# Seven-product units: one product over all of K at a time, with partial results passed from PSUM bank to PSUM bank

## The chip, the cores and the metric

The kernel runs on one core of one Trainium2 chip. Its engines work side by side and meet only at semaphores: PE (TensorE, matmuls; PEld is its weight load), DVE (VectorE) and ACT (ScalarE) for elementwise work, POOL (GpSimd) and SP (SyncE), which here issue transfers. SBUF is the working memory, PSUM the eight banks that matmuls add into, each 128 partitions x 512 float32. The metric is device time in microseconds (us): the median of the runs of one kernel.

## The reference

One encoder layer on x of 512 tokens x 2048, in float32. `h = rmsnorm(x)` is projected by `w_in` (2048 x 6176) to attention and gated-linear-attention operands; the two mixers' outputs go through `w_out` and are added to x; then a gated feed-forward part and a last norm:

```python
h = rmsnorm(x, attn_norm_w[l])
proj = h @ w_in[l]
aq, ak, av, gq, gk, gv, gr, glr = jnp.split(proj, split_idx, axis=-1)
...
x = x + mixed
h = rmsnorm(x, ffn_norm_w[l])
x = x + (jax.nn.silu(h @ w_gate[l]) * (h @ w_up[l])) @ w_down[l]
return rmsnorm(x, final_norm_w)
```

`w_gate` and `w_up` are 2048 x 5632. The change touches how 16 blocks of 256 columns of `w_in` (gates, GLA queries and keys, attention queries and keys) and the 44 blocks of 256 columns of `w_gate` and `w_up` are multiplied.

## The kernel before

**Numbers.** A float32 operand is split into a rounded high part (ACT, a cast to fp32r) and the rest (DVE, a subtraction). A product is high x high + high x low + low x high.

**Units of seven products.** A unit gives 256 output columns x 512 tokens. Tokens are cut into two halves of 256, columns into two halves of 128, and K = 2048 into eight pairs of 128-row tiles, so each pair is a 2 x 2 block product; Winograd's form does it with seven products instead of eight, on sums and differences of blocks. The token side (`B11`, `T1`, `T2`, `B21`, `T3`, `B22`, `T4`, for each of the eight pairs, high and low side by side) is made once and stays in SBUF. The weight side is made for every unit. One product of one pair is a wide matmul (512 columns: the high weights times the high and low tokens, L1603) and a narrow one (256 columns: the low weights times the high tokens, L1589), 112 matmuls a unit. There are 58 such units: 16 in `Front` (the first projection) and 42 in `Feed` (gate and up in turn; its first two units, u = 0 and 1, go by another, narrower form).

**Pieces.** A unit runs over K in four pieces of two pairs. Per piece, one 512 KB load of 4 x 128 rows x 256 columns (1024 bytes to a row, L1474 on SP), three DVE operations for block sums (L1493 to L1495), two casts (L1506) and two subtractions (L1511), 768 and 1024 elements; then all seven products for the piece. Seven PSUM banks take one product each, and all four pieces add into them. In `Feed` one piece in eight has its sums made ahead: generator `ahead` makes them between the matmuls of the out-projection (DVE, L1563) and writes them to HBM (`sd`, L1565, POOL), and they are read back in place of the sums (L1573).

**Eviction.** After the fourth piece `evac7` reads the seven banks: nine ACT copies and seven DVE additions and subtractions of 256 columns, then the remaining additions as four accumulating transfers on POOL (L1648, L1649, L1654, L1655), and a last DVE addition. `finish` multiplies by the norm's row, in `Front` writes the result to HBM from POOL (`grd`, `gfd`, `qkd`, L1757), in `Feed` applies silu to the gate and multiplies it with up, and writes `gd` (L1699), once for two units.

**Order and buffers.** The program's text sets each engine's order; nothing is rescheduled. Generators put into `urgent` are moved on by one step each time `run_urgent` is called, between pieces. SBUF is handed out in numbered slots: `s2` (names a0 to a35, 2 KB to a partition) and `s4` (b0 to b32, 4 KB). `put` returns a slot at the end of a first-in, first-out list and `get` takes the first, when the program is written, so who uses a slot next is fixed, and the next user waits at a semaphore for the last one. A slot that is being written out to HBM can be taken at once, and its next user then waits for that transfer. A wait stands in an engine's queue, and what is behind it waits too. The token operands fill much of `s4` in `Front`.

## Time and profile before

| | us |
|---|---|
| median of 3 runs | 2141.43 (2138.18 to 2142.17) |
| the profiled execution | 2140.3 |
| its span | 2138.5 |
| PE busy | 2126.0 |
| DVE busy | 1826.6 |
| ACT busy | 1264.8 |
| POOL busy | 388.7 |

The span runs from the first instruction to the last; the profiled execution's own time is 1.8 us longer. A row of a timeline shows start, length, engine, line, operation and output<-input with buffer numbers left out, then how many, and in brackets the idle time ahead of it with what ended it. A row of a grouped view shows the count, the busy time, the mean ns of one, and the idle time ahead of the group with what ended most of it. A row of waits shows us in total, times, and the longest. A row of DMA issues shows the size of one in KB and the median us from issue to landing. "L" and a number is a line of the kernel that the row is of.

### The profile page before, as it was taken

The numbers are of one execution on the slowest core, as the hardware profiler recorded it, in microseconds if no ns is written. First come the engines' busy times: TensorE is split into PE (matmuls) and PEld (weight loads), VectorE is DVE, ScalarE is ACT, GpSimd is POOL, SyncE is SP. The second block draws the span as 40 slices with busy tenths as digits, with TensorE's granted clock in tenths as the row PEclk, the third lists the DMA queues.
The fourth block names the chain that finished last, engine by engine and source line by source line (L and its number), as shares of the span: only waits on it lengthen the run. The fifth ranks groups of instructions, "written<-read, shape, count | busy, mean of one in ns | idle before, by whom it ended". The sixth has DMA issues, their size and how long they took to land.

```text
span 2138.5 us, 32543 instructions
## 1 busy us (share of the span) xinstructions
PE 2126.0 (99%) x11410; PEld 1825.3 (85%) x11410; DVE 1826.6 (85%) x3002; ACT 1264.8 (59%) x2281; POOL 388.7 (18%) x531
## 2 busy tenths in 40 slices
PE   9999999999999999999999999999999999999998
PEld 7888888888888889888888888888888888888887
DVE  5699999888878788899899898998999888887885
ACT  8445555477776546455555555555555666666762
POOL 0011121332222010011221122112121220332000
PEclk9999999999999999999999999999999999999999
DMA  6367777877676773477767777677667897999572
GB/s 205 128 184 181 180 180 184 203 219 212 189 228 209 244 253 108 140 177 183 190 174 184 185 180 186 178 179 196 176 181 187 247 277 248 201 255 249 188 249 79
DMA packets 272369, 416.85 MB, mean 195 GB/s; under 512 B 19853, under 2 KB 164477, under 8 KB 272206
## 3 DMA queue, kind: packets, MB, share of 16 engines
q1 hardware_dynamic: 208926, 280.10, 40.9%
q0 software_dynamic: 62960, 134.15, 29.4%
q8 instruction: 90, 1.47, 0.3%
q14 instruction: 73, 0.60, 0.1%
q10 hardware_dynamic: 320, 0.53, 0.1%
HBM read 289.57 MB, written 71.93 MB: 169 GB/s over the span
## 4 chain that ended last, share of the span: by engine, by line
PE 56%; DVE 1%; DMA 1%; ACT 1%; issue 0%; SPq 0%; DVEq 0%; ACTq 0%
PE ps L1603 25%; PE ps L1589 13%; PE ps L2024 5%; PE ps L2023 5%; PE ps L2025 5%; PE ps L347 1%; PE ps L348 1%; PE ps L346 1%; PE ps L2240 1%; PE ps L2239 1%; PE ps L2238 1%; DMA a<-xd 0%; DMA gd<-b 0%; ACT b L237 0%; DVE a L1847 0%
## 5 line engine op out<-in xcount | busy, mean ns | idle before, releaser
L1506 ACT CAST b<-b 128x1024 fp32r<-128x1024 f32 (+1 forms) x473 | 433.7, 945 | 293.5 <-DVE b L1511 199.9
L1603 PE MATMUL ps<-b,b 128*128 128x512 f32 x1760 | 517.2, 393 | 0.4 <-ACT b L1506 0.2
L1511 DVE TENSOR_TENSOR b<-b,b 128x1024 fp32r<-128x1024 f32 (+1 forms) x473 | 495.7, 1084 | 18.8 <-ACT b L1506 8.9
L1603 PE MATMUL ps<-a,b 128*128 128x512 f32 x1488 | 436.4, 393 | 0.6 <-DVE b L1623 0.6
L1603 PEld LDWEIGHTS ps<-b,b 128*128 128x128 f32 x1760 | 298.1, 188 | 33.2 <-ACT b L1506 0.7
L1589 PEld LDWEIGHTS ps<-b,b 128*128 128x128 f32 x1760 | 289.9, 190 | 42.4
L1589 PE MATMUL ps<-b,b 128*128 128x256 f32 x1760 | 318.0, 280 | 0.0
L1589 PEld LDWEIGHTS ps<-a,b 128*128 128x128 f32 x1488 | 246.6, 189 | 39.2 <-DVE b L1511 0.5
L1603 PEld LDWEIGHTS ps<-a,b 128*128 128x128 f32 x1488 | 248.9, 188 | 25.7 <-ACT b L1506 0.8
L1589 PE MATMUL ps<-a,b 128*128 128x256 f32 x1488 | 267.5, 280 | 0.1
L1999 DVE TENSOR_TENSOR b<-b,b 128x1024 fp32r<-128x1024 f32 x112 | 136.5, 1221 | 31.8 <-ACT b L1991 30.0
L1493 DVE TENSOR_TENSOR b<-b 128x512 f32<-128x512 f32 x212 | 145.2, 685 | 2.4 <-DMA grd<-b 0.9
L346 PE MATMUL ps<-b,b 128*128 128x512 f32 x332 | 134.8, 406 | 0.0
L1991 ACT CAST b<-b 128x1024 fp32r<-128x1024 f32 x112 | 116.6, 1052 | 30.1 <-DVE b L1979 16.4
L348 PE MATMUL ps<-b,b 128*128 128x512 f32 x332 | 130.0, 392 | 0.0
L347 PE MATMUL ps<-b,b 128*128 128x512 f32 x332 | 129.9, 391 | 0.0
L1648 POOL DMA_DIRECT2D b<-a x58 | 50.2, 866 | 413.2 <-ACT b L1506 272.1
L1654 POOL DMA_DIRECT2D b<-a x58 | 50.1, 864 | 285.9 <-DMA b<-a 160.9
L1494 DVE TENSOR_TENSOR b<-b,b 128x256 f32<-128x256 f32 x212 | 90.1, 425 | 7.4
L1495 DVE TENSOR_TENSOR b<-b,b 128x256 f32<-128x256 f32 x212 | 90.2, 425 | 7.3
L218 DVE TENSOR_TENSOR b<-b,b 128x512 fp32r<-128x512 f32 x116 | 77.0, 685 | 20.7 <-ACT b L237 20.5
L1629 ACT COPY a<-ps 128x256 f32<-128x256 f32 x58 | 21.6, 372 | 122.0 <-PE ps L1589 121.8
(313 smaller groups left out, 4215.5 us busy)
## 6 DMA issues: line engine op xcount, KB each, us to landing
b<-in_w_gate_dram SPq DMA_DIRECT2D x109, 512.0 KB, 4.0
b<-in_w_in_dram SPq DMA_DIRECT2D x94, 512.0 KB, 4.0
b<-in_w_up_dram SPq DMA_DIRECT2D x88, 512.0 KB, 3.9
b<-in_w_down_dram SPq DMA_DIRECT2D x88, 512.0 KB, 8.0
b<-a POOLq DMA_DIRECT2D x174, 256.0 KB, 4.5
b<-in_w_out_dram SPq DMA_DIRECT2D x32, 512.0 KB, 4.6
md<-a POOLq DMA_DIRECT2D x56, 256.0 KB, 6.9
gd<-b POOLq DMA_DIRECT2D x22, 512.0 KB, 3.9
```

The costliest lines, as they stand in the source:

```text
L346: mm(o, xh.t[:, c], wh.t[:, w], start=first and not on, stop=False, skip_group_check=on)
L347: mm(o, xh.t[:, c], wl.t[:, w], start=False, stop=False, skip_group_check=on)
L348: mm(o, xl.t[:, c], wh.t[:, w], start=False, stop=last, skip_group_check=on)
L1493: dve.tensor_tensor(s_[:, :, 0:2], r[:, :, 1:3], r[:, :, 0:1].to_broadcast(shape), op=OP.add)
L1506: act.copy(o, src)
L1511: dve.tensor_tensor(o, src, h, op=OP.subtract)
L1589: mm(o, wl, xh, start=False, stop=end, skip_group_check=True)
L1603: mm(o.rearrange("p (s t) -> p s t", s=2), wh, x_, start=first and p == 0, stop=False, skip_group_check=True)
L1991: act.copy(hi.t, self.src[i].t)
L1999: dve.tensor_tensor(lo.t, s.t, hi.f, op=OP.subtract)
L2023: mm(o, xh[:, t], wh, start=new and j == 0, stop=False, skip_group_check=True)
L2024: mm(o, xh[:, t], wl, start=False, stop=False, skip_group_check=True)
```

## The change

**A unit over K.** `Units` replaces the pieces in `Front` and in the 42 units of `Feed`. A unit is seven steps, one product each, and each step runs over all eight pairs: eight wide matmuls, then eight narrow ones, on one bank. The order of products is `B11`, `T1`, `T2`, `B21`, `T3`, `B22`, `T4`.

**Weights by quadrant.** A load (`fetch`, L1531) brings one quadrant of the unit's weights, one of the two row tiles of every pair and one half of the columns: 512 KB, in rows of 512 bytes. Up to eight are held, as long as more than `KEEP` = 3 slots of `s4` stay free. Four DVE additions of 1024 elements a unit make the sums (`add`, L1538), and each step has one cast (`cast`, L1563, ACT) and one subtraction (`sub`, L1569, DVE) of 1024 elements, two steps ahead of its matmuls (`AHEAD`).

**Banks.** The banks are X, V, Y, W and Z. X takes product 0. While PE runs product 1 into V, ACT writes -X into bank Y, and product 2 adds to it; ACT then writes -Y into bank W, DVE writes V - Y into bank Z, and products 4 and 6 add to W, 5 to Z, 3 to X. A bank that no matmul of these units has filled before gets one extra wide matmul first (`seat`). V is copied to SBUF (L1632). A step's eviction (`evac_`) stands in the program behind the casts and sums of the next step. The results are copied by ACT and added by DVE (L1623, L1624) as each bank ends, so the accumulating transfers are gone, and so are `evac7`, `ahead` and `sd`. `Front` now needs all eight pairs of token operands at its start. The products of a unit, the two halves of the result, `finish` and its writes stay.

```diff
@@ pair operands: slots kept by name, so that they can be freed by product @@
-            xi[q] = dict(x_, slots=slots + more)
+            xi[q] = dict(x_, slots=slots)
...
-        class Feed(Blocks):
...
-            def ahead(self):
...
-            def products(self, i, banks):
...
-            def evac7(self, u, banks):
...
+        class Units:
+            ORDER = ("B11", "T1", "T2", "B21", "T3", "B22", "T4")
+            FREES = {0: "B11", 4: "T3", 5: "B22", 6: "T4"}
+            AHEAD, KEEP = 2, 3
+            def open(self, first):
+                self.steps = [(u, n) for u in range(first, len(self.units)) for n in range(7)]
+                self.todo = deque((u, b) for u in range(first, len(self.units)) for b in (2, 0, 1, 3))
+                self.quads, self.sums_, self.his, self.both = {}, {}, {}, {}
+                self.banks, self.outs, self.parts = {}, {}, {}
+                self.late_ = []
+            def fetch(self, most=8):
+                while self.todo and len(self.quads) < most and len(s4.free) > self.KEEP:
+                    u, b = self.todo.popleft()
+                    r = self.quads[u, b] = s4.get(F32, [P, NP, P])
+                    w, col = self.place(u)
+                    k, h = divmod(b, 2)
+                    rows = w[:, col + h * P:col + (h + 1) * P].rearrange("(q k p) c -> k p q c", k=2, p=P)
+                    sp.dma_start(out=r.t, in_=rows[k])
+            def add(self, i):
+                if i >= len(self.steps):
+                    return
+                u, n = self.steps[i]
+                tt = lambda o, x_, y_: dve.tensor_tensor(o.t, x_.t, y_.t, op=OP.add)
+                Q = lambda b: self.quads[u, b]
+                if n == 0:
+                    s_ = self.sums_[u, 1] = s4.get(F32, [P, NP, P])
+                    tt(s_, Q(2), Q(0))
+                if n == 1:
+                    tt(Q(0), Q(0), Q(1))
+                if n == 2:
+                    s_ = self.sums_[u, 2] = s4.get(F32, [P, NP, P])
+                    tt(s_, Q(0), Q(2))
+                if n == 5:
+                    s_ = self.sums_[u, 2]
+                    tt(s_, s_, Q(3))
+                    put(self.quads.pop((u, 3)))
+            def from_(self, i):
+                u, n = self.steps[i]
+                home, key = ((self.quads, 1), (self.sums_, 1), (self.sums_, 2), (self.quads, 3), (self.quads, 0),
+                             (self.sums_, 2), (self.quads, 2))[n]
+                return home, (u, key)
+            def cast(self, i):
+                if i < len(self.steps):
+                    home, key = self.from_(i)
+                    hi = self.his[i] = s4.get(F32R, [P, NP, P])
+                    act.copy(hi.t, home[key].t)
+            def sub(self, i):
+                if i < len(self.steps):
+                    home, key = self.from_(i)
+                    hi, lo = self.his.pop(i), s4.get(F32R, [P, NP, P])
+                    dve.tensor_tensor(lo.t, home[key].t, hi.f, op=OP.subtract)
+                    self.both[i] = hi, lo
+                    if i % 7 not in (2, 3):
+                        put(home.pop(key))
+            def lead(self, i):
+                if i == 0:
+                    self.add(0)
+                self.cast(i)
+                self.add(i + 1)
+                self.sub(i)
+            def seat(self, i):
+                full = ps.free[0] in ps.full
+                b = ps.get()
+                if not full:
+                    w, x_ = self.both[i][0].t[:, 0], self.xs[0]["B11"]
+                    mm(b.t.rearrange("p (s t) -> p s t", s=2), w, x_, start=True, stop=True)
+                ps.full.add(b.i)
+                return b
+            def products(self, i):
+                u, n = self.steps[i]
+                hi, lo = self.both.pop(i)
+                k = "XVYXWZW"[n]
+                new = n < 2
+                if new:
+                    b = self.banks[u, k] = ps.get()
+                    ps.full.add(b.i)
+                o = self.banks[u, k].t
+                for q in range(NP):
+                    mm(o.rearrange("p (s t) -> p s t", s=2), hi.t[:, q], self.xs[q][self.ORDER[n]],
+                       start=new and q == 0, stop=False, skip_group_check=True)
+                for q in range(NP):
+                    mm(o[:, 0:256], lo.t[:, q], self.xs[q][self.ORDER[n]][:, 0], start=False, stop=q == NP - 1,
+                       skip_group_check=True)
+                put(hi, lo)
+                self.late_.append(i)
+            def evac_late(self):
+                late, self.late_ = self.late_, []
+                for i in late:
+                    self.evac_(i)
+            def evac_(self, i):
+                u, n = self.steps[i]
+                B = lambda k: self.banks[u, k]
+                a, z = slice(0, 256), slice(256, 512)
+                tt = dve.tensor_tensor
+                def out(k, c):
+                    o = self.outs[u].t.rearrange("p f t -> p (f t)")[:, c * 256:(c + 1) * 256]
+                    act.copy(o, B(k).t[:, a])
+                    tt(o, o, B(k).t[:, z], op=OP.add)
+                    put(self.banks.pop((u, k)))
+                if n == 0:
+                    b = self.banks[u, "Y"] = self.seat(i + 1)
+                    act.activation(b.t, B("X").t, AF.Copy, scale=-1.0)
+                if n == 1:
+                    y = self.parts[u] = s2.get()
+                    act.copy(y.t, B("V").t)
+                    put(self.banks.pop((u, "V")))
+                if n == 2:
+                    b = self.banks[u, "W"] = self.seat(i + 1)
+                    act.activation(b.t, B("Y").t, AF.Copy, scale=-1.0)
+                    b = self.banks[u, "Z"] = self.seat(i + 1)
+                    tt(b.t, self.parts[u].t, B("Y").t, op=OP.subtract)
+                    put(self.banks.pop((u, "Y")))
+                if n == 3:
+                    self.outs[u] = s4.get(F32, [P, 2, 512])
+                    out("X", 0)
+                if n == 4:
+                    y = self.parts.pop(u)
+                    tt(y.t, y.t, B("W").t, op=OP.add)
+                    o = self.outs[u].t.rearrange("p f t -> p (f t)")
+                    tt(o[:, 768:1024], y.t[:, a], y.t[:, z], op=OP.add)
+                    put(y)
+                if n == 5:
+                    out("Z", 1)
+                if n == 6:
+                    out("W", 2)
+                    c_ = self.outs.pop(u)
+                    urgent.append(self.finish(u, c_, c_.t.rearrange("p f t -> p (f t)")))
...
         class Front(...)
             def run(self):
-                banks = {}
-                for i, (u, q) in enumerate(self.seq):
...
+                for i, (u, n) in enumerate(self.steps):
+                    self.fetch()
+                    self.lead(i + self.AHEAD)
+                    self.evac_late()
...
+                    self.products(i)
...
                     run_urgent()
...
-        state["sums"] = ff.ahead()
+        state["sums"] = iter(())
```

**What moves.** First ACT, inside the first projection, from the end of one unit into the next. Names are output<-input with numbers: b is an `s4` slot (first number) and its use, a an `s2` slot, ps a bank; DMASW is a transfer from POOL, DMAHW one from SP. Before, from the casts of a unit's first piece:

```order
L1506 CAST b18_355_3115<-b9_340_2973 128x768 [waits DMAHW1_49,DVE_49]
L1506 CAST b30_356_3116<-b8_347_3045 128x1024
L1506 CAST b9_361_3169<-b17_346_3015 128x768 [waits DMAHW2_49,DVE_49]
L1506 CAST b8_362_3170<-b14_354_3111 128x1024 [waits DVE_49]
L1506 CAST b17_367_3211<-b10_352_3057 128x768 [waits DMAHW3_49,DVE_49]
L1506 CAST b14_368_3212<-b29_360_3165 128x1024 [waits DVE_49]
```

and in the changed program, where b6_248 is the previous unit's result:

```order
L1623 COPY b6_248_2239<-ps0_66_2213 128x256 [waits PE_49]
L1563 CAST b26_258_2334<-b28_230_2106 128x1024 [waits DMAHW7_49,PE_49]
L1629 ACTIVATE ps2_69_2338<-ps1_68_2313 128x512 [waits PE_49]
L1563 CAST b6_260_2357<-b14_220_2030 128x1024 [waits DMASW7_49,DVE_49]
L1632 COPY a9_67_2362<-ps3_70_2340 128x512 [waits PE_49]
L1563 CAST b14_264_2384<-b18_253_2285 128x1024 [waits DVE_49]
L1636 ACTIVATE ps7_71_2388<-ps2_69_2338 128x512 [waits PE_49]
```

Casts, copies to SBUF and copies from bank to bank (L1629, L1636) now alternate, and the cast into b6_260 has a wait for a transfer from POOL, the write of b6_248.

DVE at the same place in the changed program (L1799 is the multiplication in `finish`):

```order
L1624 TENSOR_TENSOR b6_248_2239<-b6_248_2239,ps0_66_2213 128x256 [waits Activation_49]
L1799 SCALAR_TENSOR_TENSOR b6_248_2239<-b6_248_2239,a28_45_650 128x1024 [waits DVE_49]
L1569 TENSOR_TENSOR b32_259_2336<-b28_230_2106,b26_258_2334 128x1024 [waits DMAHW7_49,PE_49,Activation_49]
L1538 TENSOR_TENSOR b18_253_2285<-b18_253_2285,b28_230_2106 128x1024
L1569 TENSOR_TENSOR b22_261_2360<-b14_220_2030,b6_260_2357 128x1024 [waits PE_49,Activation_49]
L1569 TENSOR_TENSOR b5_265_2386<-b18_253_2285,b14_264_2384 128x1024 [waits PE_49,Activation_49]
L1638 TENSOR_TENSOR ps6_72_2390<-a9_67_2362,ps2_69_2338 128x512 [waits Activation_49]
```

The subtraction L1569 of one step and the cast of the next share a slot: b14_220 is read by the fifth row, and b14_264 is the cast's output that the sixth row reads.

ACT at the start of the first projection in the changed program; L617 evicts the V part of the job ahead of it, in four quarters, which POOL writes to `vd`:

```order
L617 ACTIVATE b17_105_1068<-ps4_29_737,small_76 128x8x64 [waits DVE_49,PE_49]
L617 ACTIVATE b29_106_1072<-ps1_30_738,small_76 128x8x64 [waits PE_49]
L617 ACTIVATE b8_107_1076<-ps2_31_739,small_76 128x8x64 [waits PE_49]
L617 ACTIVATE b17_108_1080<-ps3_32_740,small_76 128x8x64 [waits DMASW5_49,DVE_49]
L1563 CAST b29_109_1084<-b9_103_1040 128x1024 [waits DMASW6_49,DVE_49]
L1563 CAST b17_111_1105<-b19_87_941 128x1024 [waits DMAHW3_49,DMASW0_49,DVE_49]
L1629 ACTIVATE ps6_34_1109<-ps5_33_1088 128x512 [waits PE_49]
```

The fourth eviction takes the slot of the first (b17) and waits for its write to `vd`; the two casts behind it wait for the writes of the second and the fourth quarter.

SP in the gate and up stage of the changed program; b12_739 is a result that POOL writes to `gd`:

```order
L1531 DMA b28_750_8817<-in_w_gate_dram 128x8x128 [waits DMASW2_49,DMAHW0_49,DVE_49,Activation_49]
L1531 DMA b12_751_8819<-in_w_gate_dram 128x8x128 [waits DMAHW1_49,DMASW5_49]
L1531 DMA b18_758_8872<-in_w_gate_dram 128x8x128 [waits DMAHW2_49,DVE_49]
L1531 DMA b20_761_8897<-in_w_up_dram 128x8x128 [waits DMAHW3_49,DVE_49]
L1531 DMA b1_771_8996<-in_w_up_dram 128x8x128 [waits DMAHW4_49,DVE_49,PE_49]
```

Here the slot of the written result (b12) goes to a load, and the wait for POOL's transfer stands on SP.

More of the change, by code (lines that the diff above doesn't have):

```diff
@@ L1661, in evac @@
+                        mm(o, wl, xh, start=False, stop=last and p == 1, skip_group_check=True)
+                put(rh, rl, sh, sl)
             def evac(self, u, banks):
@@ L1766, in run @@
             def run(self):
[L1767 to L1786 removed]
+                assert len(xi) == NP
```

245 lines of the change are left out of this document (72 added, 173 removed).

## The prediction

> **What bounds the kernel now.** I read the page's first part, busy time by engine:
>
> ```profile
> span 2138.5 us, 32543 instructions
> PE 2126.0 (99%) x11410; PEld 1825.3 (85%) x11410; DVE 1826.6 (85%) x3002; ACT 1264.8 (59%) x2281; POOL 388.7 (18%) x531
> ```
>
> PE is busy for all but 12.5 us. "Busy" can hide slack, since matmuls overlap, so the next views are the busy time by stage (cut where the first projection and the gate and up stage begin and end) and PE's waits in those stages:
>
> ```profile
> core 0: us, PE busy (x) PEld busy (x) DVE busy (x) ACT busy (x) POOL busy (x), PEclk, DMA share, GB/s
> 105.00:425.00 320.00, 319.25 (x1823) 278.50 (x1822) 290.95 (x462) 167.03 (x278) 67.18 (x88) 1.00 0.75 185
> 425.00:845.00 420.00, 418.60 (x2237) 354.03 (x2236) 340.66 (x735) 279.98 (x619) 92.76 (x169) 1.00 0.69 212
> 845.00:1670.00 825.00, 824.50 (x4806) 726.51 (x4805) 753.78 (x1172) 454.14 (x759) 151.56 (x180) 1.00 0.69 178
> PE ps L1603 <- DVE b L1623: 0.8, 2, 0.6
> ```
>
> In the two stages that change (first and third row) PE stands still for 0.75 and 0.50 us, its clock is fully granted (1.00), and its longest wait in total is 0.8 us. DVE is at 91% there, DMA at 0.69 to 0.75. So whatever the change takes off DVE, POOL and the queues is off the path, and a gain can only come from matmuls that follow each other faster.
>
> How fast do they follow? A piece of the timeline, PE alone, start and length; first in a piece where wide and narrow matmuls alternate by two, then in one where they run in rows:
>
> ```profile
> 1206.41 0.63 PE L1603 MATMUL ps<-a,b 128*128 128x512 f32 x2
> 1206.88 0.40 PE L1589 MATMUL ps<-a,b 128*128 128x256 f32 x2
> 1207.11 0.63 PE L1603 MATMUL ps<-b,b 128*128 128x512 f32 x2
> ...
> 1211.29 0.63 PE L1603 MATMUL ps<-a,b 128*128 128x512 f32 x2
> 1211.76 2.89 PE L1603 MATMUL ps<-b,b 128*128 128x512 f32 x12
> 1214.49 0.40 PE L1589 MATMUL ps<-a,b 128*128 128x256 f32 x2
> 1214.72 1.60 PE L1589 MATMUL ps<-b,b 128*128 128x256 f32 x12
> 1216.16 0.40 PE L1603 MATMUL ps<-a,b 128*128 128x512 f32 x1
> ```
>
> Alternating, two wide and two narrow take 1207.11 - 1206.41 = 0.70, and 28 matmuls 4.90. In rows, 14 wide and 14 narrow take 1216.16 - 1211.29 = 4.87: the first two wide 0.235 each, the other twelve 0.2275, narrow ones 0.12. A unit of 112 is 2 x 4.90 + 2 x 4.87 = 19.5 us.
>
> **The change, part by part.** *Products by K.* A unit keeps 56 wide and 56 narrow matmuls. A product is now 8 wide and 8 narrow in rows: 2 x 0.235 + 6 x 0.2275 + 8 x 0.12 = 2.79 us, and seven are 19.5. Price of the order: nothing, over all 58 units. There are 8 extra matmuls (L1587 of the changed kernel, wide) that open banks: 8 x 0.235 = 1.9 us, on the path.
>
> *Taken away.* 58 x 4 accumulating transfers from POOL, and the sums made ahead (21 writes to HBM, 21 reads, 84 DVE operations). All of it lies beside a PE that did not wait for it; Of PE's 12.5 idle us, 2138.5 - 1670 - 459.77 = 8.7 lie in the last stage, which the change leaves alone, and about 1 at the start; so it is worth 0 to -3 us, and I take 0. The busy row of that last stage:
>
> ```profile
> 1670.00:2140.00 470.00, 459.77 (x2071) 381.77 (x2069) 376.41 (x501) 296.60 (x477) 73.72 (x87) 0.99 0.78 222
> ```
>
> *Weights by quadrant.* 512-byte rows where there were 1024-byte ones. No transfer of this shape is in the trace. A 512 KB load of 1024-byte rows lands in 4.0 us, and the slowest weight load of this size, `w_down`'s, in 8.0. Up to eight quadrants are held, two units' worth, so a load is issued about one unit, 19.5 us, ahead of its use: hidden at 4 and at 8. I take 0.
>
> ```profile
> b<-in_w_in_dram SPq DMA_DIRECT2D x94, 512.0 KB, 4.0
> b<-in_w_down_dram SPq DMA_DIRECT2D x88, 512.0 KB, 8.0
> ```
>
> *DVE per unit.* What one operation occupies is read from start to start, as these follow each other without a gap:
>
> ```profile
> 203.34 1.22 DVE L1756 TENSOR_TENSOR b<-b,a 128x1024 f32<-128x1024 f32 x1
> 204.47 0.69 DVE L1493 TENSOR_TENSOR b<-b 128x512 f32<-128x512 f32 x1
> ...
> 208.00 0.69 DVE L1623 TENSOR_TENSOR b<-b,a 128x512 f32<-128x512 f32 x1
> 208.61 0.68 DVE L1493 TENSOR_TENSOR b<-b 128x512 f32<-128x512 f32 x1
> ...
> 209.78 0.42 DVE L1495 TENSOR_TENSOR b<-b,b 128x256 f32<-128x256 f32 x1
> 210.13 2.08 DVE L1511 TENSOR_TENSOR b<-b,b 128x768 fp32r<-128x768 f32 x2
> ```
>
> So 1.13 for 1024 elements, 0.61 for 512, 0.35 for 256. A unit now has four sums and seven subtractions of 1024 (12.4), the closing multiplication (1.1), two of 512 (1.2) and four of 256 (1.4): 16.1 us against 19.5 on PE. Without waits DVE would have 3.4 us to spare.
>
> *Waits in the first projection: the term that decides.* The changed ACT order has, in 14 of the 16 units, a cast (L1563) whose output slot is the one that the previous unit's result was written out of; it waits for that write. Only three slots are kept free here (KEEP), so the slot comes round after three requests. Before, no wait of ACT's casts for such a write shows among the waits of this stage. The write's price:
>
> ```profile
> 223.66 1.22 DVE L1754 SCALAR_TENSOR_TENSOR b<-b,a 128x1024 f32<-128x1024 f32 x1
> 225.17 0.56 POOL L1757 DMA_DIRECT2D gfd<-b  x1 [5.67 <-DVE b L1754]
> ...
> qkd<-b POOLq DMA_DIRECT2D x8, 512.0 KB, 3.9
> ...
> grd<-b POOLq DMA_DIRECT2D x4, 512.0 KB, 3.5
> gfd<-b POOLq DMA_DIRECT2D x4, 512.0 KB, 3.1
> ```
>
> POOL starts 225.17 - (223.66 + 1.22) = 0.29 after the multiplication, and the write lands 3.1 to 3.9 after that; I take `grd`'s 3.5, between the two. Behind the waiting cast on ACT stand the copy of V, the next cast, and the copy that seeds W's bank; PE's fifth product waits for the last of these. DVE has two operations that don't need the cast (2.26 us), and then stands still until the write has landed and the cast is done:
>
> ```profile
> L1506 ACT CAST b<-b 128x1024 fp32r<-128x1024 f32 x233 | 245.4, 1053 | 52.7 <-DVE b L1511 42.8 <-DMA gd<-b 5.2 <-PE ps L348 1.4
> ACT b L1506 <- DVE b L1511: 103.8, 88, 4.1
> L2061 ACT COPY ps<-b 128x512 f32<-128x512 f32 x24 | 13.3, 590 | 2.5 <-DMA b<-md 2.5
> ```
>
> 0.29 + 3.5 + 1.05 - 2.26 = 2.6 us. Twice more per unit a cast's slot is the one that the subtraction just ahead frees (the DVE waits in the ACT order), so that cast and subtraction follow each other instead of overlapping: 1.05 once in full and once less a 256-element addition, 0.7; together 1.75. That such waits cost about a cast each is in the second row: 103.8 us in 88 times, 1.18 each, in this stage already (there hidden by PE's lead). DVE's circle is then 16.1 + 2.6 + 1.75 = 20.5 us a unit. It closes on itself through the write, so it, and not PE's 19.5, sets the pace: 1.0 us a unit, times 14, 14 us. With the write at 3.1, 0.6 a unit and 8 us; at 3.9, 1.4 and 20. The small waits between engines (a few hundredths each, some ten a unit) come on top, so I take 16.
>
> ACT's queue is the lever. By the Trainium skill ("PSUM — Partial Sum Buffer", Engine vs sequencer instructions) the queues of ACT, DVE and POOL are strict FIFO. By that rule the sum is the 16 us; if later copies could pass the waiting cast, only the cast itself would be late, by less than its product's start, and the term would be 0. The trace bears the rule out below, where ACT sits idle for gd's writes. By "DMA: Bandwidth & Descriptors" (Anatomy of one DMA) a transfer costs 2.0 us and its bytes at 436 GB/s, an estimate of 3.2 us for 512 KB, with which the term would be 3 to 4 us smaller; the rows' 3.1 to 3.9 lie on both sides of it.
>
> *The stage's start.* The fourth quarter of V is evicted into the slot of the first, whose write it now waits for (ACT row L617 in the order), then written itself, and the second cast of the stage waits for that.
>
> ```profile
> 104.55 0.53 POOL L618 DMA_DIRECT2D vd<-b  x1 [40.91 <-DVE b L615]
> 105.29 1.85 POOL L618 DMA_DIRECT2D vd<-b  x3 [0.21 <-issue]
> ...
> 104.62 0.62 PE L1603 MATMUL ps<-b,b 128*128 128x512 f32 x2
> ...
> DMA to landing us min/median/max: 2.9/5.2/20.2
> ```
>
> Rows of POOL's writes, of PE's first product, and the landing times of V's writes. The first write lands at 104.55 + 2.9 = 107.5 at the earliest; eviction on ACT and DVE (0.7 each) and POOL's 0.29 make the fourth write start at 109.2 and land at 112.1; with the cast 1.05 and the bank copy 0.59 the third product starts at 113.7. Due is 104.6 + 2 x 2.79 + 0.2 = 110.4. Price 3.3; with 4.5 a write, 6.5. I take 4.
>
> *Gate and up.* The same write exists (`gd`, every second unit), and the trace already shows ACT waiting for it without PE waiting:
>
> ```profile
> who waited for it (us, times):
>   ACT b L1506: 26.9, 8
> ```
>
> That is 3.4 us each. In the changed order the slot goes to a load of weights instead, so it is SP that waits for the write, and what stands behind on SP are loads that are needed a unit later: the cover is that lead of 19.5 us. I take 0; bound above 42 x 1.1 = 46 us if the first projection's circle held here too.
>
> **Sum**, against the profiled execution (2140.3 us, span 2138.5): 16 + 4 + 1.9 - 1 (the waits of 0.75 that were there) = +21. Its own time lies 1.1 under the median of the runs shown, 2141.43; on the median's scale 2162.
>
> **The rivals.** *PE's slack absorbs it (not slower).* Casts run two products ahead, 5.6 us, and a wait of 3.8 fits in that; the `gd` rows speak for it. Against it: the wait returns in every unit, and DVE's 3.4 us to spare are less than the 4.35 of waits, so a lead once spent is not won back. Only if two of the three waits overlap does it hold: 2141.4 + 2 = 2143.
>
> *Faster rows of matmuls.* If narrow matmuls in a row of eight on one bank ran at half of 0.2275, 0.114, a product would be 2.74 and 58 x 7 x 0.05 = 20 us go: 2121 without waits. Against it: twelve narrow ones in a row stand above at 0.12.
>
> *The circle in all units.* Every unit now hands banks from ACT to PE twice. If gate and up paid 16 / 14 = 1.1 us a unit as well: 2162 + 42 x 1.1 = 2208. For it: DVE's sum is the same there. Against it: the wait for the write is SP's there.
>
> **How the numbers follow.** Waits in the first projection alone 0.72, absorbed 0.12, faster rows 0.05, all units 0.11. The likeliest gives 2162; its own range is 2141.4 + 8 + 3.3 + 1.9 = 2154 to 2141.4 + 20 + 6.5 + 1.9 + 4 for the small waits = 2174. The range goes down to 2143, the absorbed case, and up to 2178; it leaves out the two outer rivals, 0.16. About 0.2%, 4 us, can be told from no change. Faster: 0.06 (the faster rows and a little of the absorbed case). Same: 0.11, most of the absorbed. Slower: 0.83.
>
> **What would show it.** Right: in the changed profile PE's idle time sits in the first projection, some 1 to 1.5 us a unit at one or two products of the seven; ACT's L1563 waits for `gfd`, `grd` and `qkd` writes, 2 to 4 us each, some 14 times; the stage from gate to up shows PE full; loads at L1531 keep nobody waiting. Wrong: PE waits in gate and up; or the third product of the first unit starts without a wait; or the stage of 16 units takes 16 x 19.5 = 312 us as before.

## The result, and the profile after

The changed kernel takes 2162.99 us (median of 4 runs, 2162.29 to 2165.34); the kernel before, on the same chip, 2140.9 (2138.18 to 2142.17). The ratio is 1.0107, 95% interval 1.0089 to 1.0124: slower by 22 us. The profiled execution is the one of 2165.34, 25.0 above that of the kernel before (2140.3), so what is read from the traces adds up to some 3 us more than the medians give. First the page's busy time by engine, and the windows of the three stages, cut 25 us later than before where the stages now lie:

```profile
span 2163.6 us, 30507 instructions
PE 2135.8 (99%) x11418; PEld 1835.3 (85%) x11418; DVE 1724.6 (80%) x2345; ACT 1229.1 (57%) x2051; POOL 172.6 (8%) x278
```

```profile
core 0: us, PE busy (x) PEld busy (x) DVE busy (x) ACT busy (x) POOL busy (x), PEclk, DMA share, GB/s
105.00:450.00 345.00, 328.62 (x1839) 284.74 (x1838) 267.00 (x294) 157.77 (x219) 14.75 (x28) 1.00 0.46 133
450.00:870.00 420.00, 418.40 (x2248) 355.38 (x2247) 312.30 (x654) 280.08 (x622) 77.61 (x142) 1.00 0.48 150
870.00:1695.00 825.00, 824.54 (x4791) 728.51 (x4790) 707.78 (x779) 431.37 (x600) 11.17 (x21) 1.00 0.42 121
```

DVE is busy 102 us less over the span, POOL 216 less, and the DMA share of the first stage is down from 0.75 to 0.46. None of it is time saved. In the first projection PE now stands still for 345 - 328.62 = 16.4 us, where it was 0.75; in gate and up it is as full as before. From first matmul to the next stage's first, by the timelines, the first projection takes 441.85 - 106.31 = 335.5 us (before 417.67 - 104.62 = 313.0), gate and up 1719.64 - 896.65 = 823.0 (before 1693.91 - 873.60 = 820.3). That is +22.5 and +2.7; all other stages together change by 0.1. The first is more than the added idle time, as a gap costs more than it shows: narrow matmuls start every 0.12 us but each counts as busy for 0.28, so part of a wait lies under the end of the last one (a unit with a gap of 0.85 is 1.1 longer), and the clock adds 1.7 at the stage's start (below).

What PE waits for, and in the first projection (100 to 450) what ACT's casts and DVE's subtractions wait for (total, times, longest):

```profile
PE ps L1601 <- DVE a L1645: 11.1, 12, 1.1
PE ps L1601 <- ACT ps L1629: 4.0, 2, 3.5
PE ps L1601 <- ACT ps L1636: 1.7, 2, 1.4
```

```profile
ACT b L1563 <- DVE b L1569: 92.0, 56, 2.4
DVE b L1569 <- ACT b L1563: 55.4, 42, 4.0
...
ACT b L1563 <- DMA qkd<-b: 17.7, 5, 4.1
...
ACT b L1563 <- DMA grd<-b: 14.6, 4, 5.2
ACT b L1563 <- DMA gfd<-b: 13.3, 4, 3.3
```

The casts wait 13 times for the write of the unit before, 45.6 us, 3.5 each. One unit of it, from the seventh product of one to that of the next, in order of time:

```profile
254.39 2.08 PE L1601 MATMUL ps<-a,b 128*128 128x512 f32 x8 [0.85 <-DVE a L1645]
...
258.09 1.22 DVE L1569 TENSOR_TENSOR b<-b,b 128x1024 fp32r<-128x1024 f32 x1 [0.78 <-ACT b L1563]
...
259.68 1.22 DVE L1799 SCALAR_TENSOR_TENSOR b<-b,a 128x1024 f32<-128x1024 f32 x1
...
261.20 0.53 POOL L1802 DMA_DIRECT2D gfd<-b  x1 [20.11 <-DVE b L1799]
...
264.18 1.05 ACT L1563 CAST b<-b 128x1024 fp32r<-128x1024 f32 x1 [3.34 <-DMA gfd<-b]
...
265.25 1.23 DVE L1569 TENSOR_TENSOR b<-b,b 128x1024 fp32r<-128x1024 f32 x1 [2.08 <-ACT b L1563]
...
267.60 1.23 DVE L1569 TENSOR_TENSOR b<-b,b 128x1024 fp32r<-128x1024 f32 x1 [1.11 <-ACT b L1563]
...
274.21 0.68 DVE L1645 TENSOR_TENSOR a<-a,ps 128x512 f32<-128x512 f32 x1
...
275.03 1.16 PE L1601 MATMUL ps<-a,b 128*128 128x512 f32 x4 [0.85 <-DVE a L1645]
```

The period is 275.03 - 254.39 = 20.64 us. DVE waits 0.78 + 2.08 + 1.11 = 3.97 of it, each time for a cast, never for PE, and works the other 16.67. So its circle is closed: the multiplication (L1799), the write, the cast that needs the written slot, its subtraction, and through DVE's queue the addition of W (L1645), for which PE stands still ahead of the seventh product. The stage's start, and PE after it with the granted clock of that stretch:

```profile
108.28 0.53 POOL L621 DMA_DIRECT2D vd<-b  x1 [0.83 <-DVE b L618]
109.25 0.69 ACT L617 ACTIVATE b<-ps,small 128x512 fp32r<-128x512 f32 x1 [2.05 <-DMA vd<-b]
...
111.02 0.53 POOL L621 DMA_DIRECT2D vd<-b  x1 [2.21 <-DVE b L618]
...
114.18 1.04 ACT L1563 CAST b<-b 128x1024 fp32r<-128x1024 f32 x1 [2.42 <-DMA vd<-b]
...
115.77 1.59 PE L1601 MATMUL ps<-a,b 128*128 128x512 f32 x4 [3.51 <-ACT ps L1629]
```

```profile
115.77 3.30 PE L1601 MATMUL ps<-a,b 128*128 128x512 f32 x8 [3.51 <-ACT ps L1629]
118.86 1.53 PE L1604 MATMUL ps<-a,b 128*128 128x256 f32 x8
120.23 0.62 PE L1587 MATMUL ps<-b,b 128*128 128x512 f32 x2
...
117.00:120.00 3.00, 3.00 (x12) 2.51 (x12) 1.89 (x3) 1.20 (x2) 0.00 (x0) 0.54 0.33 81
```

V's fourth quarter waits for the first quarter's write, the cast for the fourth's, and PE 3.5 us for the copy behind it. After that wait the granted clock is down to 0.54, and the third product takes 120.23 - 115.77 = 4.46 us where the others take 2.79. The start thus costs 3.5 + 1.7 = 5.2 us.

The loads by quadrant keep nobody waiting: the list of who waited for L1531 is empty. From issue they take 4.1 us, beside 4.0 for rows twice as long, though with less other traffic (see the last section):

```profile
L1531 SPq DMA_DIRECT2D b<-in_w_in_dram x64: 367/368/1687, 71.6 to 396.1; - x64
...
who waited for it (us, times):
...
DMA to landing us min/median/max: 3.7/4.1/7.2
```

### The profile page after: what moved, and what is told of

The parts are those of the page before. It is cut to its first block, busy times and chain, and to the rows that moved or that the text cites. A ratio compares the mean times of both kernels' runs of the same rounds, so it can differ in the third digit from the quotient of the medians.

```text
span 2163.6 us, 30507 instructions
## 1 busy us (share of the span) xinstructions
PE 2135.8 (99%) x11418; PEld 1835.3 (85%) x11418; DVE 1724.6 (80%) x2345; ACT 1229.1 (57%) x2051; POOL 172.6 (8%) x278
## 4 chain that ended last, share of the span: by engine, by line
PE 83%; issue 13%; DMA 1%; DVE 1%; ACT 1%; POOL 0%; DVEq 0%; SPq 0%; POOLq 0%; ACTq 0%
PE ps L1601 26%; PE ps L1604 14%; PE ps L349 6%; PE ps L350 6%; PE ps L348 6%; PE ps L2057 5%; PE ps L2056 5%; PE ps L2055 5%; PE ps L699 1%; PE ps L2270 1%; PE ps L2272 1%; PE ps L2271 1%; PE ps L643 1%; PE ps L724 1%; PE ps L723 1%
## 5 line engine op out<-in xcount | busy, mean ns | idle before, releaser
L1569 DVE TENSOR_TENSOR b<-b,b 128x1024 fp32r<-128x1024 f32 x406 | 495.2, 1220 | 133.9 <-ACT b L1563 122.0
L1563 ACT CAST b<-b 128x1024 fp32r<-128x1024 f32 x406 | 425.9, 1050 | 200.7 <-DVE b L1569 92.0
L1601 PE MATMUL ps<-a,b 128*128 128x512 f32 x1656 | 427.0, 393 | 16.4 <-DVE a L1645 11.1
L1601 PE MATMUL ps<-b,b 128*128 128x512 f32 x1592 | 421.2, 393 | 0.5 <-ACT ps L1629 0.5
L1601 PEld LDWEIGHTS ps<-a,b 128*128 128x128 f32 x1656 | 304.8, 189 | 81.9 <-issue 13.2
L1601 PEld LDWEIGHTS ps<-b,b 128*128 128x128 f32 x1592 | 280.2, 189 | 43.2 <-ACT ps L1629 0.7
L1538 DVE TENSOR_TENSOR b<-b,b 128x1024 f32<-128x1024 f32 x232 | 282.6, 1218 | 1.3 <-PE ps L350 0.7
L1604 PEld LDWEIGHTS ps<-b,b 128*128 128x128 f32 x1592 | 232.6, 190 | 23.4
L1604 PE MATMUL ps<-a,b 128*128 128x256 f32 x1656 | 242.9, 283 | 0.0
L1604 PE MATMUL ps<-b,b 128*128 128x256 f32 x1592 | 242.8, 282 | 0.0
L1604 PEld LDWEIGHTS ps<-a,b 128*128 128x128 f32 x1656 | 225.2, 192 | 8.5
L1623 ACT COPY b<-ps 128x256 f32<-128x256 f32 x174 | 64.6, 371 | 223.5 <-PE ps L1604 223.5
L2031 DVE TENSOR_TENSOR b<-b,b 128x1024 fp32r<-128x1024 f32 x112 | 136.5, 1220 | 34.8 <-ACT b L2023 34.8
L348 PE MATMUL ps<-b,b 128*128 128x512 f32 x344 | 139.8, 407 | 0.0
L350 PE MATMUL ps<-b,b 128*128 128x512 f32 x344 | 135.1, 393 | 0.0
L349 PE MATMUL ps<-b,b 128*128 128x512 f32 x344 | 134.9, 392 | 0.0
L2023 ACT CAST b<-b 128x1024 fp32r<-128x1024 f32 x112 | 116.6, 1052 | 26.6 <-DVE b L2011 15.3
L1624 DVE TENSOR_TENSOR b<-b,ps 128x256 f32<-128x256 f32 x174 | 72.2, 415 | 27.7 <-ACT b L1623 27.7
L2055 PE MATMUL ps<-b,a 128*128 128x512 f32 x240 | 93.4, 389 | 0.0
L2056 PE MATMUL ps<-b,a 128*128 128x512 f32 x240 | 93.4, 389 | 0.0
L2057 PE MATMUL ps<-b,a 128*128 128x512 f32 x240 | 93.4, 389 | 0.0
```

What stands on the lines that cost most here:

```text
L348: mm(o, xh.t[:, c], wh.t[:, w], start=first and not on, stop=False, skip_group_check=on)
L349: mm(o, xh.t[:, c], wl.t[:, w], start=False, stop=False, skip_group_check=on)
L350: mm(o, xl.t[:, c], wh.t[:, w], start=False, stop=last, skip_group_check=on)
L1538: tt = lambda o, x_, y_: dve.tensor_tensor(o.t, x_.t, y_.t, op=OP.add)
L1563: act.copy(hi.t, home[key].t)
L1569: dve.tensor_tensor(lo.t, home[key].t, hi.f, op=OP.subtract)
```

## The experiments

Each group of runs has its own runs of the kernel before beside it, so the last column is the comparison to read. Line numbers in the experiments lie a few higher than in the changed kernel. Waits of ACT and DVE in the experiments are those from 150 to 420 us.

| kernel | median us | before beside it | ratio, 95% interval | us over before |
|---|---|---|---|---|
| the change | 2162.99 | 2140.9 | 1.0107 (1.0089 to 1.0124) | 22.1 |
| hold | 2147.29 | 2139.82 | 1.0034 (1.0021 to 1.0046) | 7.5 |
| ping | 2149.55 | 2139.82 | 1.0043 (1.0028 to 1.0058) | 9.7 |
| keep4 | 2142.97 | 2139.82 | 1.0011 (1.0002 to 1.0020) | 3.2 |
| feed_alone | 2142.88 | 2139.82 | 1.0010 (1.0001 to 1.0020) | 3.1 |
| dve | 2179.97 | 2141.12 | 1.0180 (1.0165 to 1.0196) | 38.9 |
| hold_d1 | 2164.07 | 2141.12 | 1.0109 (1.0092 to 1.0126) | 23.0 |
| keep4_d1 | 2147.45 | 2141.12 | 1.0030 (1.0019 to 1.0041) | 6.3 |
| keep4_d2 | 2167.46 | 2141.12 | 1.0124 (1.0109 to 1.0139) | 26.3 |
| keep5_d2 | 2145.39 | 2139.61 | 1.0024 (1.0015 to 1.0033) | 5.8 |
| keep5_d3 | 2153.19 | 2139.61 | 1.0061 (1.0047 to 1.0074) | 13.6 |
| keep5_alt | 2140.18 | 2139.61 | 1.0001 (0.9992 to 1.0010) | 0.6 |
| copy_first | 2162.25 | 2139.61 | 1.0103 (1.0090 to 1.0117) | 22.6 |

**hold: the wait for the write taken away.**

```diff
+                self.held = []
...
                     pool.dma_start(out=grd[u] if u < 4 else ..., in_=c)
-                    put(c_)
+                    if u < len(self.units) - 1:
+                        put(*self.held)
+                        self.held = [c_]
+                    else:
+                        put(c_)
...
+                put(*self.held)
```

> In the first projection the slot that a unit's result was written out of is given back one unit later, so that no cast of the next unit is put into it; the computation and the order of instructions stay. Theory (DVE's circle of 16.1 us work, 2.6 for the write, 1.75 for two cast-and-subtract pairs over one slot): without the write the circle is 17.9 us, under PE's 19.5, so all of the per-unit loss goes, about 13 x 1.05 us and the 1.5 of the first such unit, and the stage's start (3.7 us) stays: 2163 - 15 = 2148, with PE's gaps of 1 us a unit gone. Rival, the pairs over one slot alone make the loss: at most the write's share of it goes, and 2155 to 2163 is measured. Rival, the hand-over of banks between ACT, DVE and PE, or the order of the rows, makes the loss and the slots have no part in it: 2163.

The per-unit loss is gone. PE's waits (none is left for the addition of W), and the pairs of cast and subtraction, which are still there:

```profile
PE ps L1601 <- ACT ps L1629: 4.1, 2, 3.6
```

```profile
ACT b L1563 <- DVE b L1569: 54.7, 41, 1.9
```

The stage takes 424.17 - 105.02 = 319.15 us, 16.4 less than with the change.

**ping: the pairs over one slot taken away, the write left.**

```diff
                     if i % 7 not in (2, 3):
-                        put(home.pop(key))
+                        if self.LATER:
+                            put(*self.kept)
+                            self.kept = [home.pop(key)]
+                        else:
+                            put(home.pop(key))
...
         class Front(Units):
+            LATER = True
...
+                put(*self.kept)
```

> In the first projection the slot that a subtraction has read is given back one product later, so that the next cast is not put into the slot that the subtraction just ahead of it reads; the casts still wait for the write of the unit before (some 13 times). Theory: the circle is 16.1 + 2.6 = 18.7 us, under 19.5, so the loss per unit goes here too although the waits for the write are still in the trace: 2163 - 15 = 2148, or up to 2150 if the first unit starts later. Rival, the wait for the write alone makes the loss: it stays, 2160 to 2163. Rival, bank hand-over or row order: 2163.

Again the loss goes, though the casts still wait for the writes, 13 times and 2.5 each (first fence). PE waits for the addition of W once in the whole stage (second):

```profile
ACT b L1565 <- DMA qkd<-b: 16.5, 6, 4.4
...
ACT b L1565 <- DMA gfd<-b: 8.4, 4, 2.1
ACT b L1565 <- DMA grd<-b: 7.9, 3, 3.2
```

```profile
PE ps L1607 <- DVE a L1651: 1.0, 1, 1.0
```

So neither wait makes the loss alone; the two together do. That was the prediction's arithmetic (each sum alone under 19.5).

**keep4: one slot more in the ring.**

```diff
         class Front(Units):
+            KEEP = 4
```

> One number changed: in the first projection four slots are kept free of loads where there were three, so that a slot comes round after four requests. No cast then waits for a write, nor for the subtraction just ahead of it, and a load is issued later by one slot. Theory: the whole loss per unit goes, and about half of the stage's start, since the fourth quarter of V finds another slot: 2163 - 15 - 2 = 2146, down to 2143. Rival, bank hand-over or row order: 2163. Rival, the loads are late once one slot less is filled ahead: PE waits for loads, and the time stays above 2150.

Both the loss per unit and most of the start are gone: ACT evicts all four quarters of V in one go, and the third product waits 1.4 where it waited 3.5. The clock stays at 1.00 after this shorter wait, and the product takes 2.91 us (111.95 to 114.86), not 4.46. Against hold, which has the long wait and the low clock too, the stage is 3.8 us shorter (315.4 and 319.15).

```profile
102.80 2.73 ACT L617 ACTIVATE b<-ps,small 128x512 fp32r<-128x512 f32 x4 [7.27 <-PE ps L350]
...
111.95 1.43 PE L1601 MATMUL ps<-a,b 128*128 128x512 f32 x5 [1.37 <-ACT ps L1629]
```

The banks are handed over as in the change, and none of the per-unit loss is left, so the hand-over isn't what made it. A slot more undoes a gap of 0.8 to 1.1 us that stood once in each unit, 12 times; by the Trainium skill ("Perfetto Trace Analysis", Optimization Strategy) a gap that repeats on the engine that should be full can mean too little memory for the next tile, and this run agrees.

**feed_alone: the first projection as before, gate and up as changed** (`class Front` and its old base put back; too long for a diff).

> The first projection as it was before the change, and gate and up as the change has them. Theory: gate and up pay their four opening matmuls (0.9 us) and nothing else, and the taken-away transfers are worth 0 to 3 us: 2139 to 2143, no change against before. Rival, the circle or the order of the rows costs in gate and up too: 2.7 us longer there as in the one trace, or more, 2144 to 2150.

The total lies where the theory had it, but not for its reason. Gate and up take 823.0 us here too, as in every kernel with rows of eight in this study; the 2.7 us are real, and the opening matmuls (four here, 0.235 each) are only 0.9 of them. keep5_alt below finds most of the rest.

**dve, hold_d1, keep4_d1, keep4_d2: DVE loaded on purpose.** The value is computed a second time into the same place. `AGAIN` is set in `Front` alone (it is empty in gate and up): `(6,)` for dve and the two `_d1`, `(1, 6)` for keep4_d2.

```diff
                     dve.tensor_tensor(lo.t, home[key].t, hi.f, op=OP.subtract)
+                    if i % 7 in self.AGAIN:
+                        dve.tensor_tensor(lo.t, home[key].t, hi.f, op=OP.subtract)
```

> The changed kernel, with one subtraction of every unit of the first projection (that of its seventh operand) issued twice: 1.13 us more of DVE per unit, nothing else. Theory: DVE's work and its waits close the circle (16.6 busy and 4.0 waiting make the 20.6 of a unit in the trace), so all of it comes on top in about 15 units: 2163 + 17 = 2180. Rival, PE's own order or ACT sets the pace and DVE has 3 us a unit to spare: 2163 to 2165.

17 us slower than the change, as if nothing hid any of it: DVE's circle sets the pace of the stage. One thing besides DVE's work changed in the trace: the granted clock was 0.96 from 105 to 300 us (the change: 0.99). After a gap of 2.1 us a product took 4.41 us (238.90 to 243.31). That is made up by a shorter gap, 0.8, in the next unit: the two units together take 44.04 us (238.90 to 282.94), 22.0 each, and DVE's sum is 16.67 + 1.25 + 3.97 = 21.9. So the clock is not what makes the 17.

```profile
PE ps L1604 <- DVE a L1648: 21.3, 13, 2.3
```

> The kernel that gives the written-out slot back one unit later, with the same second subtraction. Theory as the prediction had it (a sum of DVE's work and waits over a unit): 17.9 + 1.1 = 19.0 us, under 19.5, so 2147 as without it. Rival, a limit by products: DVE's idle time in a unit (2.8 us in this kernel's trace) lies between hand-overs of banks that it may not pass, and can't be saved up for the products that have more than 2.8 us of DVE work; then up to 1.1 us a unit comes on top: 2147 + 15 to 17 = 2163.

2164, the rival's number: one subtraction of 1.1 us costs 15.5 over hold (23.0 - 7.5). The theory's sum of 19.0 was too low, since the real circle is 272.84 - 251.98 = 20.86 us. DVE's idle times in it:

```profile
251.98 2.08 PE L1604 MATMUL ps<-a,b 128*128 128x512 f32 x8 [1.07 <-DVE a L1648]
...
255.68 1.22 DVE L1570 TENSOR_TENSOR b<-b,b 128x1024 fp32r<-128x1024 f32 x1 [0.78 <-ACT b L1564]
...
263.01 1.23 DVE L1570 TENSOR_TENSOR b<-b,b 128x1024 fp32r<-128x1024 f32 x1 [1.11 <-ACT b L1564]
...
265.27 1.23 DVE L1539 TENSOR_TENSOR b<-b,b 128x1024 f32<-128x1024 f32 x1 [0.42 <-PE ps L1604]
...
269.40 0.42 DVE L1627 TENSOR_TENSOR b<-b,ps 128x256 f32<-128x256 f32 x1 [0.51 <-ACT b L1626]
...
272.84 0.70 PE L1604 MATMUL ps<-a,b 128*128 128x512 f32 x2 [1.07 <-DVE a L1648]
```

The first two are the pairs. The third is a sum whose output slot holds an operand that PE's wide matmuls (L1604) have only just read. The fourth waits for a copy (L1626) into the slot that the doubled subtraction reads. Here the copy can't be told from one that waits for its bank: the subtraction ends at 268.88, PE's product at 268.97. In hold's trace it waits for the subtraction:

```profile
ACT b L1623 <- DVE b L1569: 28.3, 12, 2.4
```

Both waits, 0.44 each, stand in hold's trace too, where they cost nothing. Giving slots back in another order has put other late users into a ring that is as short as before. Is it the ring, then, or the hand-over of banks, as the rival says? The next two runs and those with five slots bear on it.

> The kernel that keeps four slots free, with the same second subtraction. Theory of the sum over a unit: 16.6 + 1.1 = 17.7 and at most 1.0 of a wait for the write that its trace shows ahead of a subtraction: under 19.5, so 2143, or 1 us more at the stage's start. Rival, the limit by products: up to 1.1 us a unit, 2143 + 15 = 2158.

2147.5, 3.1 more than keep4 (6.3 - 3.2): above the theory's 2143 to 2144, and far from the rival's 15 more. PE waits for the addition of W twice in the stage, 2.3 us in all, and the other units follow each other at 19.68 us, where keep4's do at 19.56.

> The same with two subtractions of every unit (of its second and seventh operand) issued twice, 2.26 us more of DVE a unit. Theory of the sum over a unit: 16.6 + 2.3 = 18.9, and 19.9 with the wait for the write: 2143 to 2143 + 15 x 0.4 = 2149. Rival, the limit by products: 1.1 to 2.2 us a unit, 2160 to 2175.

2167.5, far above the theory's 2149. A wait had moved: with four slots it is a subtraction that gets the written slot, and DVE waits for the write itself, 22.2 us in 12 times, 1.9 each:

```profile
DVE b L1570 <- DMA qkd<-b: 8.1, 5, 2.1
DVE b L1570 <- DMA gfd<-b: 7.1, 4, 2.0
DVE b L1570 <- DMA grd<-b: 7.0, 3, 2.9
```

16.7 + 2.5 + 1.9 = 21.1 us is the circle, and the units do follow each other at 21.2. In keep4's own trace the same wait is 1.0 us. DVE comes to it 3.5 us after the multiplication's start in both, but the 512 KB writes land later here: a median of 3.8 to 3.9 us from issue, beside 2.9 in keep4 (`gfd`, `qkd`). Why they do isn't shown; three loads were issued during one such write here and two in keep4.

**keep5_d2 and keep5_d3: a ring without late users** (`KEEP = 5`, and two or three subtractions of seven issued twice, `AGAIN = (1, 6)` and `(1, 4, 6)`).

> In the first projection five slots are kept free, and two subtractions of every unit are issued twice (2.3 to 2.5 us more of DVE). Theory: the bound is DVE's work and waits in a unit, and with one slot more no operation of DVE or ACT meets a slot whose last user has not finished; the circle is 16.6 + 2.5 = 19.1 us, under 19.5, so the 24 us that the same two subtractions cost with four slots go: 2143 to 2148. Rival, the hand-over of banks makes DVE wait for PE at every product, and its idle time can't be used whatever the slots: 2160 to 2168 as with four.

2145.4: of the 23 us that the same load cost with four slots (26.3 - 3.2), 2.6 are left (5.8 - 3.2). The units follow each other at 19.69 us. PE's waits in this stage are that of its start (1.4) and one of 0.5; DVE's one wait in every unit is for the copy that seeds W's bank:

```profile
PE ps L1604 <- ACT ps L1632: 1.9, 2, 1.4
...
PE ps L1604 <- ACT b L1626: 0.5, 1, 0.5
...
DVE ps L1641 <- ACT ps L1639: 8.3, 14, 0.6
```

So the hand-over of banks does cost DVE 0.6 us of its spare time a unit, and PE the 0.13 by which a unit is longer than 19.56.

> The same with three subtractions issued twice, 3.4 to 3.7 us more of DVE a unit. Theory of work and waits: 16.6 + 3.4 to 3.7 = 20.0 to 20.3, 0.5 to 0.8 over PE's 19.5, in some 15 units: 2143 + 8 to 12 = 2151 to 2155. Rival, bank hand-over: 2175 or more. If it stays at 2143 to 2147, DVE's work is smaller than read.

2153.2, as 16.7 + 3.4 to 3.7 against 19.5 says. The period in the trace is 20.18 us, and from 150 to 420 us DVE has no wait at all: it works all the time, and PE waits for it. With that the rival is out as the cause of the 15 to 24 us: with a ring that is long enough two subtractions all but fit into DVE's spare time, and three do not. That hold_d1's price was one of slots as well follows from this but was not run: hold's order with a longer ring is missing.

**copy_first: the copy of V ahead of the waiting cast.**

```diff
                     self.fetch()
+                    if (n - 1) % 7 in (1,):
+                        self.evac_late()
                     self.lead(i + self.AHEAD)
```

> The changed kernel, with the copy of V (ACT's instruction right behind the cast that waits for the write) issued ahead of that cast. By the prediction's step that the queue behind the waiting cast is what is late (copy of V, next cast, seed of W's bank), a part of the per-unit loss goes: 2155 to 2161. Theory after the traces: the cast itself is what is late, since the subtraction on DVE waits for it, and the copies behind it are early enough anyway: 2163, no change.

No change (22.6 over before, and 22.1 for the change), and PE waits for the addition of W as in the change. The copy of V behind the cast is not what is late.

```profile
PE ps L1601 <- DVE a L1645: 11.2, 13, 1.1
```

**keep5_alt: two wide and two narrow matmuls in turn, with five slots** (arguments of the matmuls left out below).

```diff
-                for q in range(NP):
-                    mm(<wide, hi.t[:, q]>)
-                for q in range(NP):
-                    mm(<narrow, lo.t[:, q]>)
+                for q in range(0, NP, 2):
+                    for r in (q, q + 1):
+                        mm(<wide, hi.t[:, r]>)
+                    for r in (q, q + 1):
+                        mm(<narrow, lo.t[:, r]>)
...
         class Front(Units):
+            KEEP = 5
```

> Five slots kept free in the first projection, and in both stages a product's matmuls alternate, two wide and two narrow, where they run eight wide and then eight narrow. In the traces gate and up take 823.0 us with rows of eight in every kernel of this study and 820.3 before, of which 0.9 are the opening matmuls and 0.6 one wait. If rows of eight are slower than the mixed order of before, gate and up fall by 1 to 2 us and the kernel is at 2140 to 2142, no longer to be told from before. If the order has no price, as the prediction took it, gate and up stay at 823.0 and the kernel is at 2142 to 2144.

2140.2 beside 2139.6: not to be told from before. Gate and up take 1695.94 - 874.84 = 821.1 us, 1.9 less than with rows of eight:

```profile
874.84 0.63 PE L1602 MATMUL ps<-a,b 128*128 128x512 f32 x2
...
1695.94 0.40 PE L348 MATMUL ps<-b,b 128*128 128x512 f32 x1
```

So the order has a price, 1.9 / 294 = 6.5 ns a product. This is the best version of the study, and it does not beat the kernel before. What DVE, POOL and the queues were relieved of stays off the path, because PE is full.

## Why the prediction was right, and where not

Forecast 2162, measured 2163.0. Term by term, against before:

| step | predicted us | shown |
|---|---|---|
| waits in the first projection | 16 (8 to 20) | 16.4 (the change's stage less hold's in the traces; 14.6 by the medians) |
| the stage's start | 4 (3.3 to 6.5) | 5.2 (3.5 of waiting, 1.7 of a lower clock) |
| eight opening matmuls | 1.9 | 1.9 (there are 8 in the trace; 0.235 each is the rows' pace) |
| order of the products | 0 | about 2.6 (1.9 in gate and up by keep5_alt; 0.7 in the first projection, 315.4 for keep4 and 314.7 for keep5_alt, with one slot between them too) |
| loads by quadrant; what is taken away | 0 | 0 (nobody waits; feed_alone is not faster) |
| gate and up, the circle | 0 | 0; one wait of 0.5 at its start |

Less the 0.75 of waits that were there before, the last column adds up to 16.4 + 5.2 + 1.9 + 2.6 - 0.75 = 25.3, which is what the traces differ by (22.5 + 2.7). The forecast had 21. The main term is right by its mechanism and its size. That the total came within 1 us is luck in part: the order of the products and the clock were put at nothing, and the medians differ by 3 us less than the traces.

**The circle** was 20.5 by forecast and is 20.64, from other parts: work 16.67 and not 16.1 (operations follow each other with a few hundredths between them), DVE's wait for the written slot 2.08 and not 2.6, the pairs 0.78 + 1.11 = 1.89 and not 1.75. The write was the mis-sized term: here, with a DMA share of 0.46, 2.98 us pass between its start on POOL and the cast (264.18 - 261.20), where 3.5 was taken from rows of a stage at 0.75. By the Trainium skill ("DMA: Bandwidth & Descriptors", Anatomy of one DMA) the estimate for 512 KB was 3.2; this trace is a little below it. (With 3.2 the prediction's term falls by 0.3 us in each of 14 units, 4.2 us, and not 3 to 4.) That work and write were off in opposite ways is luck of 0.5 us a unit, some 7 us; the range would have held that.

**The step that failed** is the one on how the late cast reaches PE: "PE's fifth product waits for the last of these", the copy that seeds W's bank, and ACT's queue as "the lever". In the trace PE waits at the seventh product, for DVE, 12 times and 11.1 us in all. The fifth product waits for that seed in two units only, 1.7 us in all (L1636 among PE's waits), those in which the cast waits longest for the write (5.2 and 4.1). copy_first shows that the copy of V may go ahead of the cast without gain. (The seed of W can't be moved so far, as it needs the product in between; for it there is the trace alone.) The cast is late on its own account, and the subtraction behind it hands that on, so the sentence that the term would be 0 if later copies could pass the cast does not hold. On ACT, the rule on strict queues (the Trainium skill, "PSUM — Partial Sum Buffer", Engine vs sequencer instructions) is not tested by this. The sum rests on DVE's queue, and there the trace agrees with the rule: DVE's operations run in the order of the text, and 2.08 us pass with nothing done until the late cast is there.

**Order of the products at no price** failed by 2.6 us. The 28 alternating matmuls take 1211.29 - 1206.41 = 4.88 us by the rows shown, and not 4.90, so beside 4.87 in rows the two orders could not be told apart there; 0.007 a product is below what such rows give. The rows of 14 in that piece run over several banks, too, and not on one.

**The rivals.** "Absorbed" put DVE's spare time at 3.4 us and needed two of the three waits to overlap: hold and ping bear that out from both sides, and by the trace the spare time is 19.5 - 16.67 = 2.8, which agrees with keep5_d2 (2.5 more of work all but fits) and keep5_d3 (3.5 does not). But the sum of work and waits over a unit is a lower bound only. In hold_d1 it gave 19.0 and the unit took 20.9, as the shortened wait let others come up in the same ring. "The circle in all units" is out: gate and up have the same DVE work (707.78 us in 825, or 16.7 in 19.5), their `gd` slot goes to a load, and the list of who waited for that write is empty. "Faster rows" went the other way.

## To carry to other kernels

When buffers come round in a short ring, ask of each request who used the slot last and when that user is done; a write to HBM is the late user, and every late user that stands in one engine's circle is added to its work. Check the sum of work and waits against the pace of the bound engine; removing one wait pays only until the next late user of the same ring shows, so lengthen the ring (here one number, from 3 to 4 or 5) before reordering releases. And an engine at 80% is not free: here DVE could give up 102 us for nothing and yet set the pace of a stage.

## What the runs showed of the hardware

Wide and narrow matmuls in turn by two are faster than rows of eight by 6.5 ns in a product of 16, 1.9 us over 294 products, with the clock at 1.00 in both: the one thing here that is no wait at all.

A wait of PE can cost more than its length. After 3.5 us at the stage's start the granted clock fell in the traces of the change, hold, ping, copy_first and dve, and the next product took 4.2 to 4.5 us for 2.8; in hold_d1's trace it stayed at 1.00 after the same wait (2.90). After 1.4 us (keep4) and after 0.85 between units (the change) it stayed at 1.00.

A 512 KB load in rows of 512 bytes landed in 4.1 us, in rows of 1024 bytes in 4.0. That does not make the shorter row free, since POOL's transfers beside it had gone. In gate and up (900 to 1650 us) SP's queue took 38.0% of the DMA engines' time for 80.25 MB in the change, and 38.2% for 91.22 MB before: an eighth more for each byte, hidden here.
